# First sums of weights by a copy and an adding transfer, seven products for six pairs in every block, and PSUM banks lent one by one

## The chip, the cores and the metric

The kernel runs on one core of a Trainium2 chip. The metric is the device time of one execution in microseconds (us), the median of several runs. "Span" is the time from the first to the last instruction of one profiled execution.

## The reference, cut to what matters

The function is a two-layer encoder trunk on 256 tokens of width 4096. Each layer normalises its input, multiplies it by one wide matrix, runs an attention group and a retention group on the pieces, and multiplies the joined result by a second matrix:

```
for l in range(DEPTH):                                   # 2 layers
    h = rmsnorm(x, norm_w[l])                            # (256, 4096)
    proj = h @ w_in[l]                                   # 4096 x 11264
    aq, ak, av, ag, rq, rk, rv, rg = split(proj)
    a_out = silu(ag) * attention(rope(norm(aq)), rope(norm(ak)), av)
    r_out = silu(rg) * rmsnorm(bidirectional_retention(rope(rq), rope(rk), rv))
    x = x + concat(a_out, r_out) @ w_out[l]              # 4096 x 4096
return rmsnorm(x, final_norm)
```

Nearly all arithmetic is in the two large products of each layer, in float32.

## The kernel before

**Blocks, pairs and products.** The columns of both weight matrices are cut into blocks of 1024 (two halves of 512): 11 for `w_in` and 4 for `w_out` in each layer, 30 in all. The four matrices are the stages 0 to 3 (11, 4, 11 and 4 blocks). Along the 4096 rows there are 16 "pairs" of 256 rows. One pair of one block is a 2x2 by 2x2 product of tiles: 256 tokens (two halves of 128) by 256 rows (two of 128) by 1024 columns (two of 512). Done directly it takes eight products of tiles (an "eight"). Done by the Strassen-Winograd scheme it takes seven products, of sums of tiles (a "seven"). The table `SEVENS` says for each stage which pairs are sevens: 5, 6, 5 and 6 of 16, so 5 x 11 + 6 x 4 = 79 in a layer and 158 in all.

**What a product is.** Every float32 operand is split into a rounded high part and a low part. A product is three matmuls, with the activations as the stationary 128x128 tile and 512 columns of weights moving: high by high and high weights by low activations (L1587, weights `whi` or `bhi`, activations `x8h`, `x8l` of eights, `x7h`, `x7l` of sevens), then low weights by high activations (L1597, `wlo` or `blo`). They add up in eight PSUM banks, M1 to M8, over the whole block; at its end DVE and ACT combine the banks into two output pages, `ca` and `cb`.

**How weights are prepared.** SP loads 512 KB pages of weights into six `wraw` buffers. For each page ACT casts the high part into a ring of five buffers (`whi`), and DVE subtracts it from the page to get the low part (`wlo`, also five). An eight takes two pages, A and B, with four products each. A seven loads both pages too and makes four things of them: A as it is (two products), T (two products), the third (one product, a half page, in `bhi` and `blo`) and U (two products). T and U are the weight sums of the scheme. DVE makes T with one subtraction of 128x1024 and U with two of 128x512, all into `wsum`. In stage 3 one page of a block may be made "far": high part copied, low part written negated by ACT, and the weights added to it by an adding transfer (`flo`, three times in all).

**The order of the work.** Everything is recorded in one program with a hand-made planner. `Clock` keeps an estimated time for DVE and ACT, `Now` for PE, and `tick()`, called between matmuls, lets in the preparation of weights, the splitting of the next activations and side tasks (rotary, attention, retention, gates, outputs) where these estimates leave room. What comes out is a fixed order of instructions for each engine, joined by semaphores; each engine then takes its own in order. Numbers such as `LANDING`, `PASS` or `STEP_V` are such estimates. POOL's queue carries the transfers of the side tasks (`store`, `fetch`, the residual added to `ca` and `cb`), the few powers for square roots, and the adding transfers.

**Banks lent.** Attention and retention have their own small products, which need a PSUM bank. The four banks `SHARED` = M1, M5, M7, M6 are used by sevens alone. They are lent to side products (`take_bank`) from the block's end, when all four have been read, until four products ahead of the next block's first use of M1; then all are closed at once.

Of the kernel before, what the change touches and what calls it, by code (L numbers as in the profile page):

```python
# [12 lines left out]
F32R = mybir.dt.float32r  # L13
# [23 lines left out]
RAWS = 6  # L37

RING = 5
FAR = 1  # L40

STRICT = 9
RELIEF = 1.0
# [4 lines left out]
HALVES = 2  # L48

STEP_V = 2.0  # L50
STEP_S = 1.5
# [5 lines left out]
PASS = 0.3  # L57
# [4 lines left out]
FAR_LANDING = 11.0  # L62
MARGIN = 0.0

RUSH = 1.5
# [12 lines left out]
AT_ONCE = 2  # L78
# [7 lines left out]
SEVENS = ((3, 4, 6, 10, 11), (3, 4, 6, 10, 11, 13), (3, 4, 6, 10, 11), (3, 4, 6, 10, 11, 13))  # L86
# [13 lines left out]
HOLD = 4  # L100
# [3 lines left out]
LATE = 35  # L104

FARS = ((), (), (), (5,))

# [16 lines left out]
def constants():  # L124
# [26 lines left out]
A11, A12, S4, A22N, S1, S2, S3 = range(7)  # L151
# [8 lines left out]
    ("M4", A22N, PAGE_U, 1),  # L160
# [17 lines left out]
SPREAD = (3, 4, 7, 11, 13)  # L178
SPREAD1 = (3, 6, 8, 10, 11, 13)
SPREAD2 = (3, 4, 7, 9, 11)  # L180
SPREAD3 = (6, 7, 9, 11, 13, 14)
# [28 lines left out]
def pages_of(group, stage, first=False):  # L210
# [9 lines left out]
    turns = TURNS if group[-1] == NP - 1 else "0123"  # L220
# [3 lines left out]


def is_far(stage, p, k):

    return k == PAGE_B and p in FARS[stage]
# [25 lines left out]
TURNS = "01"  # L254
# [48 lines left out]
def hybrid_encoder(  # L303
# [39 lines left out]
    held, pledges = [0], [0]  # L343
# [21 lines left out]
    dec = t(cp, [P, DEPTH * 2 * RET_HEADS], "dec")  # L365
# [4 lines left out]
    junk = t(cp, [P, RV], "junk", dt=mybir.dt.bfloat16)  # L370
    nc.scalar.dma_start(nw, norm_wT)
# [65 lines left out]

    class Weights:


        def __init__(self):
            self.pages = []
            for l in range(DEPTH):
                for w, n in ((w_in, N_IN), (w_out, N_OUT2)):
                    for b in range(n):
                        stage = 2 * l + (w is w_out)
                        start = (l, b) == (0, 0) and w is w_in
                        for g in GROUPS[stage] if b else FIRST_GROUPS[stage]:
                            for slot in slots_of(g, stage, start):
# [4 lines left out]
                                one.far = False  # L454
                                one.can = is_far(stage, one.pair, one.kind) and not (
                                    start and (one.pair < 6 or one.whole)
                                )
                                one.src, one.begun, one.low_at, one.next = [], False, None, []
                                one.kept, one.half = None, one.seven and one.kind == PAGE_B
                                one.allowed = one.wanted = False  # L460
                                if w is w_out and (l, b) == (DEPTH - 1, n - 1) and one.pair in DELAYED:
                                    one.kept = 0 if one.kind == PAGE_A else 1
                                    one.uses, one.left = one.uses - 1, one.left - 3
                                    one.can = False
                                if one.kind == PAGE_A:
                                    one.src.append(w[l, b, one.pair, 0])
                                if one.kind == (PAGE_A if one.seven else PAGE_B):
                                    one.src.append(w[l, b, one.pair, 1])
                                self.pages.append(one)
            self.wholes = [g for g in self.pages if g.whole]  # L470
            half = [g for g in self.pages if g.half]
            for g, then in zip(half, half[HALVES:]):
                g.next.append(then)
            for g in half[:HALVES]:
                g.allowed = True
            for i, g in enumerate(self.pages):
                g.third = next(v for v in self.pages[i:] if v.half) if g.seven and g.kind == PAGE_T else None
            self.seq = [g for g in self.pages if not g.whole and not g.half]
            self.line, self.made, self.passed = [], 0, 0
            self.todo, self.credit, self.at = [], 0, 0  # L480
            self.afar, self.granted = 0, 0
            self.raw, self.later, self.adds = [], [], []

        def more(self):

            while self.passed < len(self.seq) and self.seq[self.passed].far:
                self.passed += 1
            if self.passed == len(self.seq):
                return False
            ahead = [v for v in self.seq[self.passed + AHEAD : self.passed + AHEAD + 2] if v.can and not v.far]  # L490
            if ahead and self.afar < FAR and PAGES - held[0] - pledged() >= 2 + SPARE:
                v = ahead[0]
                v.far = True
                self.afar += 1
                pledges[0] += 2
                self.line.append(v)
                self.todo += v.src
            g = self.seq[self.passed]
            self.passed += 1
            self.line.append(g)  # L500
            self.todo += g.src
            return True

        def load(self):
            while not self.todo:
                if not self.more():
                    return
            r = t(wp, [P, 2, NB], "wraw", RAWS)
            nc.sync.dma_start(r, self.todo.pop(0))
            self.raw.append(r)  # L510

        def grant(self):

            if self.granted < RING:
                self.granted += 1
                self.release(None)

        def release(self, g):

            if g and g.far:  # L520
                self.afar -= 1
                drop(2)
            elif g and g.half:
                for v in g.next:
                    self.begin(v)
            else:
                self.credit += 1
            while True:
                if self.made == len(self.line) and not self.more():
                    return  # L530
                one = self.line[self.made]
# [1451 lines left out]
```

## Time and profile before

| what | value |
|---|---|
| median of 3 runs (lowest to highest) | 2609.94 us (2609.6 to 2611.21) |
| span of the profiled execution | 2608.2 us |
| PE busy | 2594.3 us, 99% |
| DVE busy | 2313.5 us, 89% |
| ACT busy | 1662.6 us, 64% |
| POOL busy | 238.3 us, 9% |
| transfers: SP's queue, POOL's queue | 59.8% and 11.3% of the 16 DMA engines' time |

The profiled execution's own time is its span, 2608.2 us, and what lies around it (loading and ending the program), which the profile does not show; the median of the timed runs stands 1.7 us above the span. A row of the groups gives the line, the engine, the operation, the tiles out<-in, their shape and the count; then the busy time, the mean duration in ns, and the idle time of the engine just before with what ended it. Nearly every DVE and ACT row has one line, that of the helper which records them (L288 before), so groups are told apart by their tiles.

### The profile page before, as it was taken

What the parts mean: (1) busy time and instruction counts of PE and PEld (TensorE: products, weight loads), DVE (VectorE), ACT (ScalarE), POOL (GpSimd) and SP (SyncE); (2) the same over time, 40 slices, a digit from 0 to 9 for tenths busy, and PEclk for the clock granted to TensorE, in tenths of its full rate; (3) what the DMA queues carried; (4) which work ended last, traced back from release to release, by engine and by line L of the source; (5) the groups of instructions that cost most, each with busy time, mean ns of one, the idle gap of its engine ahead of it and who ended that gap; (6) DMA issues with size and microseconds to landing.
All of it is one profiled execution on the core that took longest, in us unless ns stands there. A gap on an engine that the chain in (4) does not pass through costs nothing.

```text
span 2608.2 us, 33718 instructions
## 1 busy us (share of the span) xinstructions
PE 2594.3 (99%) x11626; PEld 2148.0 (82%) x11626; DVE 2313.5 (89%) x2760; ACT 1662.6 (64%) x2413; POOL 238.3 (9%) x371
## 2 busy tenths in 40 slices
PE   9999999999999999999999999999999999999998
PEld 7888888888888888888888888888888888888886
DVE  8898988998888999888999889888998798998887
ACT  7765666666555687555795566675665457776554
POOL 0010211111001100111001101211100010000000
PEclk9999999999999999999999999999999999999999
DMA  8876867867666665787777778677675676667775
GB/s 291 281 254 234 267 213 267 273 211 245 207 208 216 240 205 195 256 274 221 264 226 235 223 235 279 211 259 264 231 245 186 215 233 232 197 201 232 243 252 168
DMA packets 181100, 612.05 MB, mean 235 GB/s; under 512 B 21952, under 2 KB 28608, under 8 KB 180928
## 3 DMA queue, kind: packets, MB, share of 16 engines
q1 hardware_dynamic: 147040, 520.17, 59.8%
q0 software_dynamic: 33168, 88.63, 11.3%
q8 instruction: 91, 1.49, 0.2%
q10 hardware_dynamic: 720, 1.10, 0.1%
q14 instruction: 81, 0.66, 0.1%
HBM read 565.77 MB, written 44.04 MB: 234 GB/s over the span
## 4 chain that ended last, share of the span: by engine, by line
PE 96%; DVE 2%; issue 1%; ACT 1%; DMA 0%; SPq 0%; DVEq 0%; POOLq 0%; POOL 0%; ACTq 0%
PE M L1587 62%; PE M L1597 31%; PE M L1070 1%; PE M L1069 1%; PE M L1068 1%; DVE wlo L288 1%; PE M L1581 0%; DVE wsum L288 0%; ACT whi L288 0%; DMA whole<-in_w_in 0%; ACT ca L288 0%; DVE ca L288 0%; DVE cb L288 0%; DVE x8l L288 0%; DVE xf L288 0%
## 5 line engine op out<-in xcount | busy, mean ns | idle before, releaser
L288 ACT CAST whi<-wraw 128x1024 fp32r<-128x1024 f32 (+1 forms) x795 | 823.9, 1046 | 501.9 <-PE M L1587 434.8
L288 DVE TENSOR_TENSOR wlo<-wraw,whi 128x1024 fp32r<-128x1024 f32 (+1 forms) x795 | 951.2, 1213 | 107.8 <-ACT whi L288 105.8
L1587 PE MATMUL M<-whi,x8h 128*128 128x512 f32 x2356 | 917.5, 389 | 0.0
L1587 PE MATMUL M<-whi,x8l 128*128 128x512 f32 x2356 | 917.1, 389 | 0.0
L1597 PE MATMUL M<-wlo,x8h 128*128 128x512 f32 x2356 | 672.1, 389 | 0.0
L1587 PEld LDWEIGHTS M<-whi,x8l 128*128 128x128 f32 x2356 | 442.3, 188 | 91.8 <-DVE x7l L288 0.2
L1587 PEld LDWEIGHTS M<-whi,x8h 128*128 128x128 f32 x2356 | 442.4, 188 | 91.5 <-ACT whi L288 0.2
L1597 PEld LDWEIGHTS M<-wlo,x8h 128*128 128x128 f32 x2356 | 441.3, 188 | 91.0
L288 ACT CAST whi<-wsum 128x1024 fp32r<-128x1024 f32 x316 | 332.4, 1052 | 262.6 <-DVE wsum L288 138.2
L1587 PE MATMUL M<-whi,x7h 128*128 128x512 f32 x1124 | 437.4, 389 | 0.0
L1587 PE MATMUL M<-whi,x7l 128*128 128x512 f32 x1124 | 437.3, 389 | 0.0
L288 DVE TENSOR_TENSOR wlo<-wsum,whi 128x1024 fp32r<-128x1024 f32 x316 | 384.8, 1218 | 33.4 <-ACT whi L288 31.9
L1597 PE MATMUL M<-wlo,x7h 128*128 128x512 f32 x1124 | 342.1, 390 | 0.3 <-DVE wlo L288 0.2
L1587 PEld LDWEIGHTS M<-whi,x7h 128*128 128x128 f32 x1124 | 211.0, 188 | 44.1 <-issue 0.4
L1587 PEld LDWEIGHTS M<-whi,x7l 128*128 128x128 f32 x1124 | 211.0, 188 | 43.7
L1597 PEld LDWEIGHTS M<-wlo,x7h 128*128 128x128 f32 x1124 | 210.1, 188 | 44.6 <-DVE wlo L288 1.6
L288 DVE TENSOR_TENSOR wsum<-wraw 128x1024 f32<-128x1024 f32 x158 | 192.1, 1216 | 1.5 <-DMA wraw<-in_w_in 1.2
L288 DVE TENSOR_TENSOR wsum<-wsum,wraw 128x512 f32<-128x512 f32 x158 | 109.4, 692 | 5.5
L288 DVE TENSOR_TENSOR blo<-wraw,bhi 128x512 fp32r<-128x512 f32 x158 | 108.0, 684 | 0.0
L288 DVE TENSOR_TENSOR wsum<-wraw,wsum 128x512 f32<-128x512 f32 x158 | 107.6, 681 | 0.4
L288 ACT CAST bhi<-wraw 128x512 fp32r<-128x512 f32 x158 | 97.1, 615 | 0.0
L288 DVE TENSOR_TENSOR cb<-cb,M 128x512 f32<-128x512 f32 x74 | 50.4, 681 | 23.8 <-PE M L1597 23.8
(232 smaller groups left out, 1935.4 us busy)
## 6 DMA issues: line engine op xcount, KB each, us to landing
wraw<-in_w_in SPq DMA_DIRECT2D x700, 512.0 KB, 4.4
wraw<-in_w_out SPq DMA_DIRECT2D x256, 512.0 KB, 4.4
full<-next_dram POOLq DMA_DIRECT2D x18, 512.0 KB, 7.1
kv<-kv_dram POOLq DMA_DIRECT2D x16, 512.0 KB, 8.1
p_dram<-room POOLq DMA_DIRECT2D x64, 128.0 KB, 3.0
pT<-p_dram POOLq DMA_DIRECT2D x16, 512.0 KB, 12.0
next_dram<-room POOLq DMA_DIRECT2D x40, 128.0 KB, 4.0
x<-in_x SPq DMA_DIRECT2D x8, 512.0 KB, 6.9
```

Of the source, the lines that this page charges most:

```text
L288: return call(out, *args, **kwargs)
L1068: nc.tensor.matmul(out, a[0], b[0], start=start, stop=False)
L1069: nc.tensor.matmul(out, a[0], b[1], start=False, stop=False)
L1070: nc.tensor.matmul(out, a[1], b[0], start=False, stop=stop)
L1587: nc.tensor.matmul(acc[name], a[i], g.hi[h], start=m == first[name] and not i, stop=False)
L1597: nc.tensor.matmul(acc[name], a, g.lo[h], start=False, stop=m == final[name])
```

## The change

**Sums of weights.** T of a seven is now w11 + w12 and w22 + w12 instead of differences, with the signs of the activations' sums and of the combine of M5 turned accordingly. ACT copies page A into `wv` (`add_up`), and a transfer issued by POOL adds the 256 KB of w12 to both halves of it, read twice from memory by a broadcast source. SP loads only w21, 256 KB, into `third`. DVE still makes U, with two operations of 128x512 (`wu`), after the adding transfer has landed. A seven's T page is begun in the planner when its sum is estimated to have landed, `ADD_LANDING` = 11 us after the copy. Page B of a seven is no longer loaded.

**Sevens.** All four stages take the six pairs 3, 5, 7, 9, 11 and 13 as sevens: 6 x 30 = 180 instead of 158. The pairs' order in the first block of each stage is spread anew.

**Buffers.** Low parts have four buffers (`LOWS`) taken when they are made, not five; `bhi` and `blo` one each, not two. Far pages are gone.

**Banks.** Each of the four shared banks is lent and closed by itself: M1 is open as soon as ACT has copied it out, and a bank closes `HOLD` = 6 products (more for a longer user, and with the engines' backlog) ahead of its own first use.

**Numbers.** The planner's estimates and limits move with these (`RELIEF`, `STEP_S`, `PASS`, `RUSH`, `AT_ONCE`, `HOLD`, `LATE`), as does the order of pages within a group (`ORDER`).

```diff
-SEVENS = ((3, 4, 6, 10, 11), (3, 4, 6, 10, 11, 13), (3, 4, 6, 10, 11), (3, 4, 6, 10, 11, 13))
+SEVENS = ((3, 5, 7, 9, 11, 13), (3, 5, 7, 9, 11, 13), (3, 5, 7, 9, 11, 13), (3, 5, 7, 9, 11, 13))
...
+RAW_LANDING = 6.0
+ADD_LANDING = 11.0
+ADD_SLACK = 0.3
...
         def begin(self, g):
...
-            elif g.kind == PAGE_A:
-                self.sums_low(PAGE_T)
-                self.a, self.b = self.taken(), self.taken()
-                self.v = t(wp, [P, 2, NB], "wsum", 2)
-                ve.tensor_sub(self.v, self.a, self.b[:, 0:1, :].to_broadcast([P, 2, NB]))
-                self.parts(g, self.a)
             elif g.kind == PAGE_T:
...
-                self.u = t(wp, [P, 2, NB], "wsum", 2)
-                ve.tensor_add(self.u[:, 0, :], self.a[:, 1, :], self.v[:, 0, :])
-                ve.tensor_sub(self.u[:, 1, :], self.u[:, 0, :], self.b[:, 1, :])
+                self.add_up(o)
+                self.add(True)
+                u = o.u = t(wp, [P, 2, NB], "wu", 1)
+                ve.after(max(o.v_at, o.b_at))
+                ve.tensor_add(u[:, 0, :], o.a[:, 1, :], o.v[:, 0, :])
+                ve.tensor_add(u[:, 1, :], u[:, 0, :], o.b)
...
+        def add_up(self, until=None):
...
+                o.v = t(wp, [P, 2, NB], "wv", SUMS)
+                ac.after(o.a_at)
+                ac.copy(o.v, o.a)
+                o.v_at = ac.until + ADD_LANDING
+                self.adds.append((ac.until, partial(nc.gpsimd.dma_start, o.v, o.added, accum_op=ALU.add)))
...
         def proceed(self, until=None):
...
+                if not until and one.seven and one.kind == PAGE_T and (o.v_at or 1e9) > max(now.t, ac.until) + ADD_SLACK:
                     return
...
     def take_bank(more=0):
...
+        def fit():
+            queue = max(0.0, ve.until - now.t, ac.until - now.t) * QUEUE
+            return [v for v in spare if v not in shut and spare[v] <= now.t and ahead[v] > HOLD + more + queue]
```

**What moves, in the order of the instructions.** Names carry buffer numbers here; `x8h_284` is the high part of pair 5's activations before, `x7h_252` the same after.

On PE, in the second block, pair 5. Before it is an eight, and its second page is 12 matmuls:

```order
L1587 MATMUL M4_2464<-whi_2645,x8h_284 128x512
L1587 MATMUL M4_2464<-whi_2645,x8l_285 128x512
L1587 MATMUL M8_2442<-whi_2645,x8h_284 128x512
L1587 MATMUL M8_2442<-whi_2645,x8l_285 128x512
L1587 MATMUL M3_2439<-whi_2645,x8h_284 128x512
L1587 MATMUL M3_2439<-whi_2645,x8l_285 128x512
L1587 MATMUL M2_2467<-whi_2645,x8h_284 128x512
L1587 MATMUL M2_2467<-whi_2645,x8l_285 128x512
L1597 MATMUL M4_2464<-wlo_2646,x8h_284 128x512
L1597 MATMUL M8_2442<-wlo_2646,x8h_284 128x512
L1597 MATMUL M3_2439<-wlo_2646,x8h_284 128x512
L1597 MATMUL M2_2467<-wlo_2646,x8h_284 128x512
```

After, it is a seven; its third and its U page end the pair with nine:

```order
L1605 MATMUL M2_2522<-bhi_2742,x7h_252 128x512
L1605 MATMUL M2_2522<-bhi_2742,x7l_253 128x512
L1615 MATMUL M2_2522<-blo_2743,x7h_252 128x512
L1605 MATMUL M6_2745<-whi_2752,x7h_252 128x512
L1605 MATMUL M6_2745<-whi_2752,x7l_253 128x512
L1605 MATMUL M4_2518<-whi_2752,x7h_252 128x512
L1605 MATMUL M4_2518<-whi_2752,x7l_253 128x512
L1615 MATMUL M6_2745<-wlo_2778,x7h_252 128x512
L1615 MATMUL M4_2518<-wlo_2778,x7h_252 128x512
```

The pair's other 12 matmuls (pages A and T of the seven, page A of the eight) stay 12, so the pair takes 21 instead of 24.

On POOL, in stage 1 (an output block), where the residual is added to `ca` and `cb` by two transfers. Before:

```order
L1030 DMA next1_dram_75<-room_9523 32x4x256 x4
L1700 DMA ca_9969<-in_x 128x2x512
L1700 DMA cb_9970<-in_x 128x2x512
L1677 DMA x2_dram_82<-ca_9969 128x1024
L1030 DMA next2_dram_76<-room_10183 32x4x256 x4
```

After, at the same place:

```order
L663 DMA wv_10285<-in_w_out 128x2x512
L1721 DMA ca_10169<-in_x 128x2x512
L1721 DMA cb_10170<-in_x 128x2x512
L663 DMA wv_10354<-in_w_out 128x2x512
L1698 DMA x2_dram_82<-ca_10169 128x1024
L1043 DMA next2_dram_76<-room_10371 32x4x256 x4
```

Two adding transfers of weights now stand around the two of the residual in one queue.

On ACT at this same place, before:

```order
L288 CAST whi_10127<-wraw_10013 128x1024
L288 CAST whi_10151<-wsum_10125 128x1024
L288 CAST bhi_10154<-wraw_10033 128x512
L288 CAST whi_10173<-wsum_10146 128x1024
L288 ACTIVATE room_10183,sums_8625<-ca_9969 128x512 x2
L288 CAST whi_10200<-wraw_10044 128x1024
```

and after:

```order
L289 CAST whi_10344<-wraw_10241 128x1024
L289 COPY wv_10354<-wraw_10283 128x1024
L289 ACTIVATE room_10371,sums_8811<-ca_10169 128x512 x2
L289 CAST whi_10384<-wv_10285 128x1024
L289 CAST bhi_10386<-third_10324 128x512
L289 CAST whi_10394<-wraw_10273 128x1024
L289 ACTIVATE room_10409,sums_8811<-cb_10170 128x512 x2
L289 CAST whi_10418<-wu_10377 128x1024
L289 CAST whi_10435<-wraw_10283 128x1024
L289 CAST whi_10455<-wraw_10316 128x1024
L289 COPY wv_10462<-wraw_10380 128x1024
L289 CAST whi_10475<-wv_10354 128x1024
```

The copy `wv_10354` stands ten rows ahead of the cast of T that reads it, `whi_10475`; the adding transfer has to land in between, and the cast waits for it on ACT's own queue.

More of the change, by code (lines that the diff above doesn't have):

```diff
@@ L76 @@
 TIGHT_B = 9
-AT_ONCE = 2
+AT_ONCE = 3
 WARM = 20
@@ L469, in __init__ @@
+                                if not one.seven or one.kind == PAGE_A:
+                                    one.src = w[l, b, one.pair, int(one.kind == PAGE_B)]
                                 self.pages.append(one)
             self.wholes = [g for g in self.pages if g.whole]
[L471 to L477, printed above, removed]
@@ L478, in __init__ @@
-            self.seq = [g for g in self.pages if not g.whole and not g.half]
[L479 to L502, printed above, removed]
```

305 lines of the change are left out of this document (171 added, 134 removed).

## The prediction

> **What bounds the kernel now.** I read the page first, then the chain, PE's waits, and PE by stretches of time.
>
> The page's head and engine lines, and the chain that ended last:
>
> ```profile
> span 2608.2 us, 33718 instructions
> PE 2594.3 (99%) x11626; PEld 2148.0 (82%) x11626; DVE 2313.5 (89%) x2760; ACT 1662.6 (64%) x2413; POOL 238.3 (9%) x371
> ...
> PE 96%; DVE 2%; issue 1%; ACT 1%; DMA 0%; SPq 0%; DVEq 0%; POOLq 0%; POOL 0%; ACTq 0%
> ```
>
> All of PE's waits in the view of waits (total, times, longest):
>
> ```profile
> PE M L1845 <- DVE half L288: 1.1, 1, 1.1
> PE M L1581 <- DMA whole<-in_w_in: 0.7, 2, 0.4
> PE M L1597 <- DVE wlo L288: 0.2, 1, 0.2
> ```
>
> Stretches of the span (length; busy time and count of PE, PEld, DVE, ACT, POOL; clock, DMA share, GB/s), and from the chain in order of time eight matmuls in a row:
>
> ```profile
> 0.00:20.00 20.00, 18.26 (x53) 8.88 (x54) 8.48 (x15) 12.30 (x21) 0.20 (x4) 1.00 0.93 351
> 20.00:40.00 20.00, 20.00 (x90) 16.52 (x89) 19.86 (x31) 15.86 (x26) 0.00 (x0) 1.00 0.82 296
> ...
> 120.00:140.00 20.00, 20.00 (x90) 16.57 (x89) 19.45 (x43) 13.79 (x31) 3.48 (x3) 1.00 1.06 258
> ...
> 473.00:710.00 237.00, 237.00 (x1079) 197.27 (x1079) 209.44 (x241) 140.65 (x181) 22.49 (x38) 1.00 0.71 236
> ...
> 2500.00:2608.00 108.00, 96.38 (x426) 79.47 (x424) 86.58 (x111) 57.29 (x81) 3.70 (x5) 0.96 0.65 213
> ```
>
> ```profile
> 539.80 1.81 PE M L1587 x8
> ```
>
> PE is the bound, at the full granted clock (1.00). Of its 13.9 us without work, 1.7 are in the first 20 us and 11.6 at the end, behind the last matmul; the change touches neither stretch's cause. In between, some 0.6 us are left, and PE waited 0.2 us for another engine. Matmuls follow each other at 1.81/8 = 0.226 us; 237 us held 1079, shorter ones of side products among them. So a matmul of 512 columns less is worth 0.2265 us, if its place is not taken by a wait; and no wait can be removed for a gain, since there is none. DVE at 89% is busy, but nothing on the path waits for it.
>
> **The change, part by part.**
>
> *Sevens, 158 to 180.* The 22 more pairs lose one product of three matmuls each: 66 x 0.2265 = 14.95 us, all on the path. This is the whole gain.
>
> *DVE and ACT.* The groups of the sums, and what a seven or an eight costs (busy, mean ns, then idle before):
>
> ```profile
> L288 ACT CAST whi<-wraw 128x1024 fp32r<-128x1024 f32 x787 | 818.9, 1051 | 500.1 <-PE M L1587 432.9 <-DMA wraw<-in_w_in 25.4 <-ACT whi L288 13.4
> ...
> L288 DVE TENSOR_TENSOR wlo<-wsum,whi 128x1024 fp32r<-128x1024 f32 x316 | 384.8, 1218 | 33.4 <-ACT whi L288 31.9
> ...
> L288 DVE TENSOR_TENSOR wsum<-wraw 128x1024 f32<-128x1024 f32 x158 | 192.1, 1216 | 1.5 <-DMA wraw<-in_w_in 1.2 <-issue 0.3
> L288 DVE TENSOR_TENSOR wsum<-wsum,wraw 128x512 f32<-128x512 f32 x158 | 109.4, 692 | 5.5
> L288 DVE TENSOR_TENSOR blo<-wraw,bhi 128x512 fp32r<-128x512 f32 x158 | 108.0, 684 | 0.0
> ```
>
> DVE loses the third of these rows, 192 us. A pair that becomes a seven costs it two sums of 0.69, the third's low part 0.68 and one low page more, 1.22: 3.28 us, 22 times 72. DVE ends near 2313 - 192 + 72 = 2193 us, 85%. ACT gains 180 copies; the nearest row is its cast of the same shape, 1.05 us, so 189 us, and 22 pairs with one cast of a page and one of half a page more, at 1.05 and up to 1.05, 46 us at most: 1662.6 + 189 + 46 = 1898 us, 73%. Both have room, and ACT's own 500 us of waiting ahead of casts is mostly for PE to free a buffer, so its copies lie beside PE. On the path: 0. If that cover were gone, the price would be what is computed for late sums below.
>
> *POOL.* 180 more issues. The nearest row is the adding transfer of `flo`:
>
> ```profile
> L598 POOL DMA_DIRECT2D flo<-in_w_out x3 | 3.1, 1024 | 1.7 <-ACT flo L288 1.7
> ```
>
> That is 184 us on an engine that is 9% busy. POOL's queue is in order, though: an add recorded behind the store of a side task starts only when that task's last DVE operation is done. Counting in the order, no add stands behind a POOL row that has to wait for a later point of PE's work than the add's own copy; so this costs 0, and at most DVE's backlog of a few us in the landing below.
>
> *DMA engines.* A 30 us stretch that holds three adding transfers in a row (2340 to 2370), its two queues, then times from issue to landing:
>
> ```profile
> q1 hardware_dynamic: 1926, 6.77, 63.7%
> q0 software_dynamic: 432, 1.57, 27.9%
> ...
> wraw<-in_w_out SPq DMA_DIRECT2D x12, 512.0 KB, 5.7
> ca<-x_dram POOLq DMA_DIRECT2D x1, 512.0 KB, 8.7
> cb<-x_dram POOLq DMA_DIRECT2D x1, 512.0 KB, 12.0
> flo<-in_w_out POOLq DMA_DIRECT2D x1, 512.0 KB, 15.0
> ```
>
> ```profile
> 2352.00:2367.00 15.00, 15.00 (x68) 12.43 (x67) 12.69 (x13) 8.21 (x10) 0.86 (x1) 1.00 1.01 273
> ```
>
> and of the whole run (first the engines' mean busy share in 40 slices of 65 us, in tenths):
>
> ```profile
> DMA  8876867867666665787777778677675676667775
> ...
> q1 hardware_dynamic: 147040, 520.17, 59.8%
> q0 software_dynamic: 33168, 88.63, 11.3%
> ...
> wraw<-in_w_in SPq DMA_DIRECT2D x700, 512.0 KB, 4.4
> ...
> ca<-x_dram POOLq DMA_DIRECT2D x3, 512.0 KB, 5.8
> ```
>
> One add takes 27.9% of 30 us / 3 = 2.8 us of all 16 engines, 1.9 times a plain load of the size (63.7% of 30 us / 12.9 = 1.48 us). SP loses 180 pages of 512 KB for 180 thirds of 256 KB, 47 MB, at 59.8% for 520 MB 5.4 points. The adds bring 180 x 2.8 = 504 us, 19.4 points of the span, less 0.3 for the three `flo`. The engines go from 71 to about 85%. In the 15 us in which three adds made them full (share 1.01), weights landed in 5.7 instead of 4.4 us and PE was busy for 15.00. With six buffers of weights in turn that is cover.
>
> *The new wait: sums that land late.* ACT's cast of T waits for the add on its own queue, and every cast behind waits too. What is left for the landing: from the point of PE's work that frees ACT's cast just ahead of the copy to the first matmul on T there are 104 matmuls at the place shown in the order, 23.6 us; that is near the median over all 180 pairs (23.0), and the least is 71, 16.1 us. Off go the copy 1.05, the cast 1.05, U's two sums ahead on DVE 1.37, T's low part 1.22: 4.7. So 18.9 us are left at this place, 11.4 at the tightest. A landing is 5.8 to 8.7 us for a transfer that is first in line, 12.0 for the second, 15.0 for the third. By the order 162 adds have under 1 MB of other POOL transfers ahead of them within 8 us of PE's work; 18 have 1 MB or more, and these keep 17.1 us or more. So none is due late by the rows. Bounds: 0, and for the six tightest pairs, third in line, 15.0 - 11.4 = 3.6 us or less, about 15 us together. I take 1.5 us, near the lower end, because the tight ones have one transfer ahead.
>
> The Trainium skill ("DMA: Bandwidth & Descriptors", Anatomy of one DMA) fits 2.0 us plus bytes over 436 GB/s to a transfer from this queue, 3.2 us for 512 KB; the rows have 5.8 to 8.7 for an adding one beside SP's loads. By the skill's figure this term would be 0 and the sum 2596.0; the rows decide.
>
> *The start.* In the first 40 us the share is 0.93 and 0.82, and two adds with their thirds bring 2 x (2.8 - 0.74) = 4.1 us of engines to the second 20 us: 20.5 of 20. ACT also does two copies more, 2.1 us, while the buffers are not yet full. Bounds: 0, and both, 0.5 + 2.1 = 2.6 us. I take 1.0, below the middle, because ACT was busy for only 12.30 of the first 20 us.
>
> *Banks, order, smaller rings.* PE waited 0.2 us for low parts and nothing for a bank: no gain to be had. Low parts in four buffers instead of five, and a second U behind one buffer, take lead away on DVE, whose load falls by 4 points: 0, with a loss bounded by the sums' term.
>
> Sum on the profiled execution: 2608.2 - 14.95 + 1.5 + 1.0 = 2595.8; the median stands 1.7 above, so **2597.5 us**. The floor, with nothing lost, is 2595.0.
>
> **Rivals.**
>
> *Late adds (slower).* Place: the 18 adds with 1 MB or more ahead, seven of them between the residual's two adds and their stores. If the line there is two places longer than I counted (the sum before has not landed, side stores in between), the landing is 15.0 + 2 x 3.1 = 21.2 against 17.1: 4.1 x 18 = 74 us, 2671. It decides from 0.9 us of lateness at each (landing 18.0), which gives back the gain. For it: two adds of weights stand around those of the residual. Against: the stretch at 2352 had the same three and lost nothing. The Trainium skill ("TensorE: Matmul & The Clock Gate", part 1) adds that an idle window of about 3.4 us halves PE's clock; the trace has no such wait in the middle, so no run here shows it.
>
> *Full DMA engines (about the same).* Six of the 40 slices of 65 us have an 8 (0.8 to 0.9). With 13.7 points more, a slice at 0.9 lacks 0.037 x 65 = 2.4 us, six 14: weights late by that would make 2612. In the Trainium skill ("DMA: Bandwidth & Descriptors", Rules for kernel authors) transfers of all queues share the same 16 engines and interleave, so the adds are taken from the weights. Against it: 20 us at 1.06 (120 to 140) cost PE nothing, and the mean stays at 85%.
>
> *Part of both.* A few tight pairs and the start lose 3 to 10 us: 2598 to 2605, 2602 in the middle.
>
> **How the numbers follow.** This kernel's runs lie within 0.06% of each other, and 0.2% (5.2 us) is about what a measurement can tell from no change. Chances: the forecast (2593 to 2600) 0.68; part of both 0.16; full engines 0.09; late adds 0.07. Faster by over 0.2% is below 2604.7: the first and nearly all of the second, 0.83. Same: 0.10. Slower: 0.07. The range goes from 2592.5, a little under the floor, by the 0.6 us that PE lacks in the middle and gaps too short for these views, to 2606, so that about 0.15 is left out above.
>
> **What would show it.** PE has 66 instructions fewer, and near 2579 us busy. DVE falls to about 85%, ACT rises to 73%, and a group `wv<-wraw` of 180 copies on ACT takes about 1.05 us each. Adds land in 6 to 15 us, POOL's queue takes about 30% of the DMA engines, SP's 54%. Right: PE still waits under 3 us for others in the middle. Wrong: PE waits for `wlo` of T pages, ACT's casts wait for DMA `wv` by tens of us and PE behind them; or casts wait for `wraw` far beyond the 25.4 us of now; or the copy costs clearly more than the cast.

## The result, and the profile after

The changed kernel took 2687.41 us (2683.35 to 2702.14), the one before 2609.93 us (2609.6 to 2611.21) beside it: a ratio of 1.0306, 95% interval 1.028 to 1.0332. The forecast was 2597.5 us, so it lost where a gain was expected, by 90 us. The profiled execution's span is 2681.6 us.

The page's head, engine lines, queues and the chain:

```profile
span 2681.6 us, 34374 instructions
PE 2613.6 (97%) x11560; PEld 2136.4 (80%) x11560; DVE 2197.0 (82%) x2702; ACT 1847.1 (69%) x2634; POOL 457.8 (17%) x548
...
q1 hardware_dynamic: 147040, 472.99, 50.2%
q0 software_dynamic: 81696, 181.44, 30.5%
...
PE 38%; DMA 5%; DVE 4%; issue 2%; ACT 1%; SPq 0%; POOL 0%; DVEq 0%; POOLq 0%; ACTq 0%
```

The chain could be followed back over only half of the span (its shares add up to 50), but in that half transfers and DVE now stand where PE alone stood. PE's largest waits (total, times, longest) and, by stretches, its busy time and the granted clock (columns as in the prediction):

```profile
PE M L1615 <- DVE wlo L289: 23.0, 30, 3.3
PE M L1081 <- ACT pr L289: 8.1, 6, 2.2
PE M L1605 <- ACT whi L289: 6.5, 5, 3.8
PE M L1605 <- DVE ca L289: 4.9, 5, 1.5
```

```profile
0.00:20.00 20.00, 18.45 (x53) 9.04 (x53) 7.39 (x14) 12.63 (x21) 1.55 (x5) 1.00 0.92 350
20.00:40.00 20.00, 16.19 (x58) 12.61 (x57) 11.66 (x21) 12.79 (x23) 1.21 (x1) 0.83 0.88 273
473.00:710.00 237.00, 229.42 (x1026) 187.42 (x1025) 200.04 (x241) 159.04 (x217) 49.28 (x64) 1.00 0.83 251
```

In the stretch from 473 PE was busy for 237.00 of 237 us before; now 7.6 us are missing. Summed over the trace's starts of matmuls, what stands above the pitch (start to start) of 0.2265 us, or half of that for the half-size ones, was 2.8 us in the run before and is 88.9 us now. The opening, whose matmuls with `whole` weights start every 0.43 us in both kernels, is left out. I call that sum PE's excess. 64 gaps of 0.3 us or more hold 65 us of it, some 50 matmuls at about half pace 10 us. So 86.1 us of excess against 14.95 us of matmuls saved: that is the 73.4 us between the spans, to within 2.3.

Who is late is seen a step ahead of PE. Groups whose idle time before them names a transfer, and times from issue to landing:

```profile
L289 DVE TENSOR_TENSOR wu<-wu,third 128x512 f32<-128x512 f32 x180 | 124.6, 692 | 187.2 <-DMA third<-in_w_in 116.2
...
L289 ACT CAST bhi<-third 128x512 fp32r<-128x512 f32 x180 | 111.6, 620 | 211.3 <-DMA third<-in_w_in 139.4
...
L289 ACT CAST whi<-wv 128x1024 fp32r<-128x1024 f32 x180 | 188.5, 1047 | 66.4 <-DMA wv<-in_w_in 27.4
...
L289 ACT COPY wv<-wraw 128x1024 f32<-128x1024 f32 x180 | 188.6, 1048 | 43.9 <-DMA wraw<-in_w_in 19.7
...
wraw<-in_w_in SPq DMA_DIRECT2D x568, 512.0 KB, 4.9
...
wv<-in_w_in POOLq DMA_DIRECT2D x132, 512.0 KB, 7.8
third<-in_w_in SPq DMA_DIRECT2D x132, 256.0 KB, 5.6
```

DVE and ACT stood for 187 and 211 us ahead of the operations that read the third, most of it for the transfer, though a third lands 5.6 us after its issue in the median. So the time of the issue matters. In order of time, SP's queue (start, length of the whole group, its issues), then DVE and ACT:

```profile
502.68 7.11 SPq L490 DMA_DIRECT2D wraw<-in_w_in  x3
509.84 0.42 SPq L507 DMA_DIRECT2D third<-in_w_in  x1
```

```profile
513.36 0.68 DVE L289 TENSOR_TENSOR wu<-wraw,wv 128x512 f32<-128x512 f32 x1
518.41 0.69 DVE L289 TENSOR_TENSOR wu<-wu,third 128x512 f32<-128x512 f32 x1 [4.37 <-DMA third<-in_w_in]
```

```profile
509.94 1.05 ACT L289 CAST whi<-wv 128x1024 fp32r<-128x1024 f32 x1
518.42 0.62 ACT L289 CAST bhi<-third 128x512 fp32r<-128x512 f32 x1 [7.43 <-DMA third<-in_w_in]
```

The third is recorded behind three page loads, each of which waits on SP's queue until DVE has released a `wraw` buffer. The waits of that queue, of before and of the changed kernel:

```profile
SPq L509 <- DVE wlo L288: 1391.2, 589, 10.1
```

```profile
SPq L490 <- DVE wlo L289: 1748.9, 558, 9.5
```

The third here is issued at 509.84 and landed at 518.3, so both its issue and its landing (8.5 us, against the median of 5.6) are late; DVE and ACT, in order as well, hold every low part and every cast behind it for 4.37 and 7.43 us. PE's next wait, at 520.29, is 0.76 us for DVE's `wlo`: the lead (what DVE and ACT have ready ahead of PE) goes first, then PE waits.

### The profile page after: what moved, and what is told of

Same layout as the page of the kernel before. It is cut to its first block, busy times and chain, and to the rows that moved or that the text cites. A ratio compares the mean times of both kernels' runs of the same rounds, so it can differ in the third digit from the quotient of the medians.

```text
span 2681.6 us, 34374 instructions
## 1 busy us (share of the span) xinstructions
PE 2613.6 (97%) x11560; PEld 2136.4 (80%) x11560; DVE 2197.0 (82%) x2702; ACT 1847.1 (69%) x2634; POOL 457.8 (17%) x548
## 3 DMA queue, kind: packets, MB, share of 16 engines
q1 hardware_dynamic: 147040, 472.99, 50.2%
q0 software_dynamic: 81696, 181.44, 30.5%
## 4 chain that ended last, share of the span: by engine, by line
PE 38%; DMA 5%; DVE 4%; issue 2%; ACT 1%; SPq 0%; POOL 0%; DVEq 0%; POOLq 0%; ACTq 0%
PE M L1605 24%; PE M L1615 12%; DVE wlo L289 3%; DMA third<-in_w_out 2%; DMA third<-in_w_in 2%; DMA wv<-in_w_in 1%; PE M L1081 1%; ACT whi L289 0%; PE M L1083 0%; PE M L1082 0%; DVE cb L289 0%; ACT ca L289 0%; DVE ca L289 0%; DVE rot L289 0%; DVE wu L289 0%
## 5 line engine op out<-in xcount | busy, mean ns | idle before, releaser
L289 DVE TENSOR_TENSOR wlo<-wraw,whi 128x1024 fp32r<-128x1024 f32 (+1 forms) x776 | 934.2, 1212 | 124.6 <-PE M L1615 64.8
L289 ACT CAST whi<-wraw 128x1024 fp32r<-128x1024 f32 (+1 forms) x776 | 797.3, 1044 | 236.9 <-PE M L1605 216.2
L663 POOL DMA_DIRECT2D wv<-in_w_in x132 | 162.6, 1232 | 1269.8 <-ACT wv L289 1009.2
L289 DVE TENSOR_TENSOR wu<-wu,third 128x512 f32<-128x512 f32 x180 | 124.6, 692 | 187.2 <-DMA third<-in_w_in 116.2
L289 ACT CAST bhi<-third 128x512 fp32r<-128x512 f32 x180 | 111.6, 620 | 211.3 <-DMA third<-in_w_in 139.4
L289 ACT CAST whi<-wv 128x1024 fp32r<-128x1024 f32 x180 | 188.5, 1047 | 66.4 <-DMA wv<-in_w_in 27.4
L289 DVE TENSOR_TENSOR wlo<-wu,whi 128x1024 fp32r<-128x1024 f32 x180 | 219.1, 1217 | 14.7 <-ACT whi L289 8.8
L289 DVE TENSOR_TENSOR wlo<-wv,whi 128x1024 fp32r<-128x1024 f32 x180 | 219.0, 1217 | 14.6 <-ACT whi L289 7.6
L289 ACT CAST whi<-wu 128x1024 fp32r<-128x1024 f32 x180 | 188.9, 1050 | 47.9 <-DVE wu L289 27.8
L289 ACT COPY wv<-wraw 128x1024 f32<-128x1024 f32 x180 | 188.6, 1048 | 43.9 <-DMA wraw<-in_w_in 19.7
```

Of the source, the lines that this page charges most:

```text
L289: return call(out, *args, **kwargs)
L663: self.adds.pop(0)[1]()
```

## The experiments

Three theories, as the expectations number or name them. One: thirds are issued too late on SP's queue. Two: the adding transfers, by being waited for or by filling the DMA engines. Three: the smaller rings, the new list of sevens and the planner's numbers leave PE less lead by themselves. Each number is a median of several runs, beside the kernel before at 2609.8 to 2610.3 us. In diffs, − is the changed kernel unless said otherwise.

**e1, thirds issued by ACT.**

```diff
-                nc.sync.dma_start(o.b, o.third)
+                nc.scalar.dma_start(o.b, o.third)
```

> The changed kernel with one edit: the loads of the thirds are issued by ACT instead of SP; the recorded order of all other work is the same. Theory 1 (a third is issued late, because on SP's in-order queue it stands behind weight loads that wait for DVE to free their buffers): DVE's 183 us and ACT's 181 us of waiting for thirds shrink to under 60 us each, and of the 89 us that PE lost most come back: 2600 to 2630 us. Theory 2 (the adding transfers fill the DMA engines, and everything lands late): unchanged, 2680 to 2695. Theory 3 (the smaller rings and the planner's numbers leave PE too little lead, whatever the thirds do): unchanged within 15 us.

2661.13 us, ratio 1.0196 (1.018 to 1.0211): 26 us back, less than theory one said and more than the other two. The waits of this run:

```profile
ACT whi L289 <- DMA wv<-in_w_in: 72.2, 31, 5.2
DVE wu L289 <- DMA wv<-in_w_in: 40.8, 19, 4.6
...
DVE wu L289 <- DMA third<-in_w_in: 13.0, 16, 1.8
```

The wait for thirds is nearly gone (116.2 to 13.0), and the wait for adds has grown in its place (27.4 to 72.2 on ACT): what was late next had been covered by the thirds.

**e2, no adding transfers.**

```diff
-                self.adds.append((ac.until, partial(nc.gpsimd.dma_start, o.v, o.added, accum_op=ALU.add)))
+                pass
```

> The changed kernel with the adding transfers left out: the sum T stays the plain copy of page A, so the output lacks w12 in T and U. 94 MB less for the DMA engines and 180 issues less on POOL, the rest in the same order. Theory 1: thirds are as late as before, 2660 to 2690 us. Theory 2: the loss is gone, 2595 to 2620. Theory 3: 2670 to 2690.

2660.5 us, 1.0193 (1.0178 to 1.0208), at the lower edge of theory one. Thirds are still waited for, if less:

```profile
DVE wu L289 <- DMA third<-in_w_in: 95.0, 34, 8.0
ACT bhi L289 <- DMA third<-in_w_in: 71.4, 21, 7.2
```

**e3, one third for all pairs.**

```diff
+    held_third = []
...
-                o.b = t(wp, [P, NB], "third", THIRDS)
-                nc.sync.dma_start(o.b, o.third)
+                if not held_third:
+                    held_third.append(t(wp, [P, NB], "third", 1))
+                    nc.sync.dma_start(held_third[0], o.third)
+                o.b = held_third[0]
```

> The changed kernel with one third loaded once and used for every seven, so the output has a wrong w21 in all others: no wait for a third at all, and 47 MB less to load. Theory 1: at or a little under the kernel whose thirds are issued by ACT, 2595 to 2620 us; what stays above 2595 is the price of something else. Theory 2: 2665 to 2685, by the bytes alone. Theory 3: 2670 to 2690.

2637.07 us, 1.0099 (1.0082 to 1.0115): 17 us above theory one's range, and well below the other two. Its runs spread from 2629 to 2640. **e5, the edits of e3 and e2 together:**

> The changed kernel with one third loaded once and used for all 180 pairs, and without the adding transfers (w12 is missing from T and U, and w21 is the first pair's everywhere); copies, sums of U, order and rings stay. All landings that DVE and ACT can wait for in their own order are gone, but for the pages themselves. If waits of DVE and ACT for late transfers are the whole loss, the time comes to the floor of 2595 us, 2600 at most, and PE's start-to-start time over 0.2265 us per matmul falls from 46 us (third once, with adds) to under 10. If the smaller rings and the new order of DVE's and ACT's work take PE's lead away by themselves, it stays at 2615 to 2637.

2613.44 us, 1.0013 (1.0004 to 1.0023). This is neither branch: most of the loss is gone, but 2600 is not reached. Its page, and its longest single wait of PE:

```profile
span 2611.4 us, 33487 instructions
PE 2587.1 (99%) x11560; PEld 2135.6 (82%) x11560; DVE 2216.5 (85%) x2702; ACT 1860.6 (71%) x2634; POOL 235.9 (9%) x368
...
PE 95%; DVE 2%; ACT 1%; issue 1%; DMA 1%; POOL 0%; SPq 0%; DVEq 0%; POOLq 0%; ACTq 0%
```

```profile
PE M L1619 <- DVE x7l L289: 3.7, 1, 3.7
```

With nothing left that can land late but the pages themselves, PE is the chain again. Excess falls from 88.9 to 20.8 us, not to under 10. **e6, the edits of e1 and e2 together,** agrees:

> Thirds issued by ACT instead of SP, and no adding transfers (w12 is missing from T and U). The thirds on ACT alone gained 26 us, the adds left out alone 27 us. If the two losses are separate and add up, 2634; if both act through one thing (whatever lands late, PE has too little lead to take it), the second removal gains more than the first alone and the time comes near 2600; if either hides the other, about 2655.

2615.39 us, 1.0021 (1.0011 to 1.0031). So thirds from ACT's queue cost 2.0 us where adds are not in the way. The sum of e1's and e2's gains would have been 2634; the two removals together gain 19 us more than that, as in the branch in which both act through one thing.

**e8, thirds early on SP.** The third is issued with the load of its pair's first page.

```diff
                 if g.seven:
                     g.own.a, g.own.a_at = g.raw, max(now.t, ve.until) + RAW_LANDING
+                    self.wanted += 1
+                    self.load_third()
...
             if g.kind == PAGE_A:
-                self.wanted += 1
-                self.load_third()
```

> The third stays on SP's queue but is issued together with its pair's first page, when that page's load is placed, instead of when the page's cast is recorded. If thirds lose because SP reaches them only after loads that wait for a buffer, the waits of DVE wu and ACT bhi for thirds (364 us together) mostly go and the time comes to that with thirds on ACT, 2661 or below. If the third's buffers (two) hold up the queue in turn, weights behind a blocked third come late and it is no better than 2687.

2658.02 us, 1.0186 (1.017 to 1.0202). The same queue, the same bytes, another place in the queue: 29 us. The waits of DVE and ACT for thirds fall from 364 to 34 us. So theory one is the place behind blocked loads, and not the queue itself.

**e9 and e17, adds that nobody waits for.** They keep the transfers and take the waiting away (the edit is cut to the line that they share; what else each leaves out stands in its expectation).

```diff
-                self.adds.append((ac.until, partial(nc.gpsimd.dma_start, o.v, o.added, accum_op=ALU.add)))
+                self.adds.append((ac.until, partial(nc.gpsimd.dma_start, spare_sum[0], o.added, accum_op=ALU.add)))
```

> One third for all pairs, as in the run that gave 2637; the 180 adding transfers are issued at the same places but add into a spare page that nobody reads (w12 is missing from T and U), and the side tasks get 12 pages instead of 13 to make room for it. The bytes and the DMA engines' time are those of the changed kernel less the thirds; no engine waits for an add. If the adds cost their 24 us by being waited for (ACT and DVE reach T about 11 us after the copy, and a landing is 5 to 17), the time is that without adds, 2613. If they cost it by filling the DMA engines, so that weights land late, it stays at 2637. Between them: both.

2718.93 us, 1.0415 (1.0394 to 1.0436). No branch of it: with 12 pages the planner put the side work of the first output blocks otherwise, and PE waited there for activations and attention:

```profile
PE M L1612 <- ACT x8h L289: 26.2, 5, 9.4
PE M L1088 <- ACT pTh L289: 23.7, 3, 12.6
```

PE's excess by place shows it (rows `e17` and `e18` are runs further down). The matmuls are cut into 30 equal parts, 0 to 29; part 11 and part 26 hold the first output block of each layer (us):

| kernel | 0 | 1-10 | 11 | 12-17 | 18-25 | 26 | 27-28 | 29 | sum |
|---|---|---|---|---|---|---|---|---|---|
| before | 0.0 | 1.6 | 0.0 | 0.0 | 1.1 | 0.0 | 0.0 | 0.0 | 2.8 |
| changed | 10.2 | 20.1 | 2.0 | 18.7 | 20.8 | 1.0 | 3.4 | 12.7 | 88.9 |
| e3, one third | 6.1 | 6.7 | 1.9 | 9.6 | 10.6 | 0.5 | 0.0 | 11.2 | 46.5 |
| e5, no adds too | 3.3 | 4.8 | 1.8 | 0.1 | 4.1 | 0.5 | 0.0 | 6.1 | 20.8 |
| e9, spare adds, 12 pages | 10.0 | 5.9 | 48.4 | 1.0 | 7.6 | 42.6 | 0.0 | 6.3 | 121.7 |
| e17, spare adds, 13 pages | 8.1 | 4.9 | 1.9 | 0.8 | 4.2 | 0.5 | 0.0 | 6.1 | 26.5 |
| e18, five low parts | 10.9 | 10.5 | 18.8 | 2.1 | 7.7 | 8.5 | 0.0 | 0.0 | 58.6 |

> The spare adds once more, with the 13 pages of side tasks of the changed kernel and its planner untouched, so that the order is that of the runs with one third: every third is a column of the norm weights, read with stride 0 (w21 is replaced by it), no third is loaded, and the 180 adds go into a page that nobody reads (w12 is missing). Against 2637 with adds that are waited for and 2613 with none: 2611 to 2618 if being waited for is the adds' whole price, 2637 if the DMA engines' load is, in between for both.

2619.45 us, 1.0036 (1.0022 to 1.005). The queues of this run, and what it does to a page's landing (e5: 4.0):

```profile
q1 hardware_dynamic: 121120, 425.79, 47.1%
q0 software_dynamic: 81696, 181.44, 31.7%
...
wraw<-in_w_in SPq DMA_DIRECT2D x568, 512.0 KB, 5.2
```

The load of the adds costs 6.0 us (2619.4 less 2613.4); being waited for costs the other 17.6 of their 23.6 (e3 less e5). Of the 5.7 us of excess between the two runs, 4.8 are in the first part and 0.9 in all the others. Away from the ends the same load costs PE next to nothing (e17, then e5; columns as above, the last but one is the engines' share):

```profile
100.00:2500.00 2400.00, 2394.00 (x10755) 1984.05 (x10754) 2057.07 (x2487) 1720.39 (x2423) 439.29 (x526) 1.00 0.79 232
100.00:2500.00 2400.00, 2394.64 (x10759) 1984.63 (x10758) 2056.82 (x2485) 1719.44 (x2421) 232.85 (x360) 1.00 0.59 196
```

Two limits: adds into one page follow each other, so two are never under way at once as they can be in the changed kernel; and since they wait for no copy, they are issued 5.4 us ahead of the copy's end in the median (from the trace's starts), not 0.4 us behind it.

**e18 and e11, five buffers of low parts.** e18 on e17's constant third, e11 on e5 and with `PAGES = 12`.

```diff
-LOWS = 4
+LOWS = 5
```

> The same constant in place of thirds, no adds (w12 and w21 missing), five buffers of low parts instead of four, 13 pages. Without thirds and adds, four buffers gave 2613.4, 18 us over the floor. If the fourth buffer's loss is what is left, 2597 to 2604; if the opening blocks and the start are, 2608 to 2614; if the one buffer more changes the planner's order at the first output blocks, as the pages did, far above, and the stretches outside of them are to be read.

> One third for all pairs and no adds (w12 missing), as in the run that gave 2613.4, with five buffers of low parts as before the change instead of four, and 12 pages for side tasks. If the smaller ring of low parts is the 18 us that this run stands above the floor, 2597 to 2602. If the order of the opening blocks or the start is, it stays at 2611 to 2616.

2651.11 us (1.0156, 1.0134 to 1.0178) and 2728.02 us (1.045, 1.0435 to 1.0466): both above, by the first output blocks and the start. What can be read is part 29: 6.1 us of excess with four buffers, 0.0 with five in both runs, and the wait of 3.7 us for `x7l` is not there. So 6 of the 18 us that e5 stands above the floor go with the fourth buffer or the order that comes with it; 3.3 are the start; the other 8.6 (18.0 less these) lie in pieces under 2 us and stay open. No run took away the lending of single banks, the planner's numbers or ACT's copies alone.

**e4 and e12, the 180 sevens with the sums on DVE.** Here − is the kernel before; e12 keeps its `SPREAD1` and `SPREAD3`.

```diff
-SEVENS = ((3, 4, 6, 10, 11), (3, 4, 6, 10, 11, 13), (3, 4, 6, 10, 11), (3, 4, 6, 10, 11, 13))
+SEVENS = ((3, 5, 7, 9, 11, 13), (3, 5, 7, 9, 11, 13), (3, 5, 7, 9, 11, 13), (3, 5, 7, 9, 11, 13))
-FARS = ((), (), (), (5,))
+FARS = ((), (), (), ())
-SPREAD = (3, 4, 7, 11, 13)
-SPREAD1 = (3, 6, 8, 10, 11, 13)
...
+SPREAD = (3, 6, 9, 10, 12, 14)
+SPREAD1 = (4, 6, 8, 9, 11, 13)
...
```

> The other half of the change alone: the kernel before, with its sums on DVE and its own numbers, takes the six pairs 3, 5, 7, 9, 11, 13 as sevens in all stages, in the new orders of the first blocks, and has no far page. PE has the same 66 matmuls less, 15 us; DVE has 22 x 4.5 = 99 us more to do, 2412 of some 2600 us, 93%. If the 22 pairs are harmless in themselves and the loss is the new path of the sums and thirds: 2595 to 2605 us. If the spread of the sevens is what starves PE: slower than 2620.

> The kernel before, with the sums on DVE, and the 180 sevens; in the first input blocks of both layers they are spread as in the change, in the first output blocks as in the kernel before (3, 6, 8, 10, 11, 13 and 6, 7, 9, 11, 13, 14). With the new spread everywhere it lost 84 us, 48 of them in the first output blocks, where PE waited for split activations. If the new spread of the output stages is the cause, 2620 to 2635, and 2597 if the rest goes with it. If the new pairs themselves are (3, 5, 7, 9, 11, 13 have their activations made later than 3, 4, 6, 10, 11, 13), it stays near 2679.

2679.43 us, 1.0266 (1.0249 to 1.0283), and 2688.53 us, 1.0302 (1.0286 to 1.0317). In e4, 48 of 83.7 us of excess lie in parts 11 and 26, where the splitting of activations comes late:

```profile
PE M L1587 <- DVE x8l L288: 21.7, 6, 7.3
PE M L1587 <- ACT x8h L288: 15.1, 5, 5.0
```

The old order there made it 57, so the opening order of the output blocks is not the cause, and neither of e12's ranges was met. **e7, the reverse,** the changed kernel with the old `SEVENS` and `SPREAD` tables:

> The changed kernel's sums, rings and planner with the 158 sevens and the opening orders of the kernel before. 66 matmuls more than in the changed kernel: +15 us by that alone. If the new sums lose by each pair (about 88 us over 180), it loses 77 us over 2610: 2687, the same as the changed kernel. If the planner's numbers and rings lose it whatever the pairs, 2690 to 2700. If the new list and order of pairs is what loses (as it does with the sums on DVE, 2679), near 2615.

2777.33 us, 1.0645 (1.0628 to 1.0662), far above every branch. Thirds and adds are later still:

```profile
L289 ACT CAST whi<-wv 128x1024 fp32r<-128x1024 f32 x158 | 165.7, 1048 | 192.5 <-DMA wv<-in_w_in 122.5
```

The old list has neighbours (3 and 4, 10 and 11) where the new sums have two buffers each for T and for thirds; that this is why was not tested. What e4 and e7 show is that list and sums can't be priced apart: each half alone loses more than 69 us, at different places. The buffers, banks and planner's numbers go with the sums in e7, so they are not priced apart either.

**e10, e13, e14, e15 and e16, a longer lead for the adds.** e10 is e8 with `SUMS = 3` and `PAGES = 12`; e13, e14 and e15 are e1, e8 and e3 with `ADD_LANDING = 15.0`; e16 is e8 with T's buffer filled by a second load of page A:

```diff
-                ac.copy(o.v, o.a)
...
+                nc.gpsimd.dma_start(o.v, o.first)
```

The lines left out drop the wait for page A and for ACT ahead of it.

e10, e13 and e14 were meant to compute the whole function, but the order that came out changes part of the result; which part was not followed up. e15 shares the setting of e13, and e9 and e11 the pages of e10. The totals of these six are not used, and their parts only where a run with 13 pages says the same or to show where the order moved.

> The changed kernel, nothing left out, with the third issued together with its pair's first page, and three buffers for T instead of two (side tasks get 12 pages instead of 13), so that a copy and its add can start a pair earlier. If lateness of the adds is what is left with early thirds (2658), a longer lead takes most of the waits for wv (167 us on DVE and ACT) away: 2610 to 2630. If the copy can't start earlier, since its page lands no earlier and the planner starts it no earlier, the waits stay and so does 2658. If full DMA engines lose it, 2658 or above.

> The changed kernel, complete, with thirds issued by ACT (that run: 2661) and the planner's landing of an add at 15 instead of 11 us, so that T's cast and U's sums stand later in the orders of ACT and DVE. If what is left there is that T and U's sums are placed 11 us behind the copy while adds take 8 to 17, the waits for wv (160 us on ACT and DVE) fall by more than half and the time to 2620 to 2640. If the lead is only moved, from the wait for the add to PE's wait for low parts of T, it stays near 2661 with more PE <- wlo.

> The same with thirds issued early on SP's queue (that run: 2658) and 15 us for an add. As for the thirds on ACT: 2620 to 2640 if the place of T in the orders is what loses, about 2658 if the lead is only moved.

> One third for all pairs (w21 of the first pair everywhere), adds as in the change, and 15 us for an add in the planner. With 11 us it was 2637, without adds 2613, so 24 us hang on the adds alone. If T's place behind the copy loses them, 2613 to 2620; if the lead is only moved, 2630 to 2640; above 2640 if the later T costs more than the wait.

> Complete, thirds early on SP. T's buffer is filled by a second plain load of the pair's first page from DRAM on POOL's queue instead of ACT's copy, as soon as the buffer is free, and then by the add: 94 MB more, 180 copies less on ACT, and a longer lead than the 11 us, since nothing waits for the page to land and for ACT. If lead is what the adds lack, the waits for wv go and the time comes to 2615 to 2635. If the DMA engines are near their limit (with these loads about 90% by the quoted shares), weights land late and it is slower than 2658.

2746.24, 2757.18, 2759.79, 2746.55 and 2756.72 us, ratios 1.0525 (1.0509 to 1.0541), 1.0561 (1.054 to 1.0582), 1.0571 (1.0554 to 1.0588), 1.0521 (1.0505 to 1.0538) and 1.0561 (1.0534 to 1.0588). In the first four a changed number of the planner moved the side work: parts 11 and 26 hold 88 of 149 us of excess in e10, and 60 to 65 of 149 to 163 in e13 to e15. Also, the median from copy to T's cast hardly moved (11.4 us in e1, 12.2 in e13), so the question of the place was not answered. In e16 the orders of parts 11 and 26 are unharmed (2.3 and 2.5), and the excess is everywhere (163.4):

```profile
q1 hardware_dynamic: 147040, 472.99, 49.5%
q0 software_dynamic: 107616, 275.82, 39.1%
...
ACT whi L289 <- DMA wv<-in_w_in: 174.4, 45, 7.7
```

The time is in the range that was given for full engines, and two transfers in a row at 89% of the engines come later than a copy and one; whether the load or the second transfer makes T late was not separated. No run beat the kernel before; e5, nearest, leaves out both transfers.

## Why the prediction was wrong

The parts found, in one order of removal: floor of the prediction 2595.0; the rest of the change with neither thirds nor adds +18.4 (e5); thirds late on SP +47.1 (e2 less e5); adds +23.6 (e3 less e5), 6.0 of it load; the remainder, both at once, +3.3. Together 2687.4. The remainder can't be told from nothing, since the runs of the changed kernel spread over 19 us and those of e2 and e3 over 10 and 11. In another order, with the bytes of the thirds kept, the late place on SP costs 45.1 (e2 less e6). And with thirds on ACT the adds cost 45.7 (e1 less e6), so their price depends on what else is late.

**Held.** PE has 66 instructions less, and e5's busy time is 8 us above the 2579 forecast; the changed kernel's own is 2613.6, 35 above. DVE 82% (85), ACT 69% (73 at most), the copy 1.048 us (1.05), the queues 50.2 and 30.5% (54 and 30). Adds land in a median of 7.9 us (6 to 15 forecast; 5.4 to 17.3 seen). All of these are sizes of work. What failed are the waits.

**The step that failed first: the thirds.** "SP loses 180 pages of 512 KB for 180 thirds of 256 KB" counted bytes and nothing else: in the sum a late third stands at nothing, without a reason, and none of the signs of being wrong names it. It cost 47.1 us. The instruction that was moved past SP's queue was not followed: what stands ahead of it there (loads that wait for DVE), and who stands behind it on DVE and ACT. The profile before had the row that should have raised it: 1391.2 us of waits of SP for DVE's `wlo`. Sums before read pages loaded long ahead (1.2 us of waits for `wraw` in the row of `wsum`); the third is loaded when its pair is begun. The Trainium skill ("DMA: Bandwidth & Descriptors", Anatomy of one DMA) says that a semaphore wait of a DMA happens on the issuing sequencer, before dispatch. The trace agrees: issue at 509.84, right behind a load that waited.

**The second: the lead of the adds.** "18.9 us are left at this place" was counted to the first matmul on T. The first reader is T's cast on ACT or U's sum on DVE, in orders in which other pages stand behind them. In e5, where no add is waited for, that reader comes 10.6 us after the copy in the median, 7.9 at the fifth percentile (from the trace's starts), against landings of 5.4 to 17.3. The rival *Late adds* had the mechanism and the wrong place: not 18 adds behind the residual, but tens of them all over (46 waits on ACT and 32 on DVE in e1).

**Third: "Banks, order, smaller rings" at 0.** What is left without thirds and adds is 18.4 us, 6 of them at the end, which go with the fourth buffer or its order, and 3.3 at the start; that the rest belongs to this term was not shown. Together this would have eaten the gain of 14.95. "With a loss bounded by the sums' term" had no row behind it.

**Also mis-sized: "The start" at 1.0 us, 2.6 at most.** Part 0 has 10.2 us of excess against 0.0 before, 8.1 with adds alone (e17) and 3.3 with neither (e5). ACT's copy there waits longer for its page (changed kernel, then e5):

```profile
27.84 1.05 ACT L289 COPY wv<-wraw 128x1024 f32<-128x1024 f32 x1 [5.47 <-DMA wraw<-in_w_in]
25.12 1.05 ACT L289 COPY wv<-wraw 128x1024 f32<-128x1024 f32 x1 [2.95 <-DMA wraw<-in_w_in]
```

The cast of T behind it ends at 33.6, and PE, which has waited 3.81 us for it, goes on at 33.69.

**The rival of full DMA engines** was priced at 14 us by slices all over the run and measured at 6.0, in e17, nearly all of it in the first part. With the adds the rest is later, too: a third lands in a median of 5.6 us and 3.9 without them (e2), and thirds on SP are waited for 364 us and 214.

## What to carry to other kernels

A gain in matmuls is kept only if every instruction of the new path is placed in time on each in-order queue it passes: for a moved transfer, name what waits ahead of it at issue, and count its lead to the first engine that reads it, not to the matmul at the end. Busy shares of DVE, ACT and the queues, all forecast well here, say nothing of that. In a kernel whose order comes from a planner, compare experiments by place and not by their totals, since one number of the planner can move other work by more than the effect looked for.

## What the hardware showed besides

A wait of PE costs more than its length. In the changed kernel, matmuls in order of time (start, duration, and the wait ahead):

```profile
28.82 1.07 PE L1615 MATMUL M<-wlo,x8h 128*128 128x512 f32 x4
33.69 0.79 PE L1605 MATMUL M<-whi,x7h 128*128 128x512 f32 x1 [3.81 <-ACT whi L289]
34.28 0.63 PE L1605 MATMUL M<-whi,x7l 128*128 128x512 f32 x1
34.71 0.63 PE L1605 MATMUL M<-whi,x7h 128*128 128x512 f32 x1
```

Behind a wait of 3.81 us matmuls start every 0.43 us instead of 0.2265, until about 39.8 us; the granted clock of those 20 us is 0.83. The Trainium skill ("TensorE: Matmul & The Clock Gate", Part 1) puts it at half rate after an idle window of about 3.4 us. The trace agrees here and at 1941 and 2658 us, behind waits of 3.3 and 3.7 us. It differs at two other places: the clock is halved for 3.4 us behind a single wait of 2.29 us, and again behind 11 us in which PE was idle for 3.06 us in pieces of 0.95 us at most:

```profile
1111.60:1115.00 3.40, 3.40 (x10) 2.64 (x9) 3.40 (x5) 2.72 (x4) 0.77 (x1) 0.50 1.04 290
1367.00:1378.00 11.00, 7.94 (x27) 4.32 (x26) 8.46 (x10) 10.83 (x17) 0.00 (x0) 0.99 0.63 164
1377.90:1381.30 3.40, 3.40 (x10) 2.65 (x9) 3.37 (x5) 3.38 (x5) 0.95 (x1) 0.51 0.51 163
```

So short waits close together can cost the same here; where the border lies was not measured. Some 50 matmuls at half pace add 10 us behind the opening.

Second, at a mean of 79% of the 16 engines (e17) instead of 58% (e5), a page of 512 KB landed in 5.2 us instead of 4.0. From 100 to 2500 us PE lost 0.6 us by it; nearly all of the 6.0 us are in the opening. At that share and past the opening the engines were not the limit that they looked like; transfers that were issued late or waited for too soon were.
